# Hymba layer on one core: the last four attention heads projected as q, k, v, z, the input loaded in four pieces, and a new step table

## The chip, the cores and the metric

The kernel runs on one core of a Trainium2 chip. The metric is the time of one execution on the device in microseconds (us); lower is better.

## The reference

One layer of a model with two token mixers side by side, for one sequence of 256 tokens and 1024 channels, in float32:

```python
h = rms_norm(x, norm_w)
proj = h @ w_in                       # q_a k_a v_a z_a | qkv_dn | z_dn | b_dn a_dn
qa, ka = rms_norm(heads(q_a)), rms_norm(heads(k_a))       # 8 heads of 64
o_a = softmax(causal(qa @ ka.T / 8 + rel_bias)) @ heads(v_a)
y_a = o_a * silu(z_a)
qkv_dn = silu(causal_depthwise_conv(qkv_dn, conv_w))      # 4 heads of 128
q_d, k_d, v_d = l2_norm(q), l2_norm(k), v
beta = sigmoid(b_dn);  g = -exp(a_log) * softplus(a_dn + dt_bias)
o_d = gated_delta_rule_chunked(q_d, k_d, v_d, g, beta)
y_d = rms_norm(o_d) * silu(z_dn)
out = x + concat(y_a, y_d) @ w_out
```

The sequence is one block of the block-sparse attention, so that each query sees its own block alone, causally. The delta rule goes over chunks of tokens; this kernel uses two chunks of 128 for each of the four heads, and needs for each the inverse of a unit lower triangular matrix.

## The kernel before

**Products.** All products with weights go through one sequence on TensorE (PE), written in `products()`. It has four stretches: `z` (8 slices of the input, 12 matmuls each: z, beta and decay columns of the delta mixer), `d` (12 chunks of 24 matmuls: q, k, v of the delta mixer), `a` (8 groups of 48 matmuls: v, q, k, z of the attention heads 0 to 3, then v, q, k, z of heads 4 to 7), and `o` (the output product, 192 matmuls). Each product is made of three fp32r matmuls: weight and input are split in a rounded part (`wh`, `xh`) and a remainder (`wl`, `xl`). ScalarE (ACT) makes the rounded parts (L195, L266), VectorE (DVE) the remainders (L196, L267). Raw weights come through a pool of 4 buffers (`wr`), the two parts have 4 buffers each, so that a chunk can be split only when PE has done with the chunk four before it.

**Steps.** Everything else is written as generators: `norm`, `gates`, `bias`, `prep` and `base` (the triangular inverse, by doubling in `levels`), `scan` (the delta rule over the two chunks of a head), `heads4` (norm and transposition of q or k of four heads, named `heads` plus segment plus half: `heads01` is q of the last four heads, `heads11` their k), and `pair` (attention of two heads: scores L689, softmax L696 to L707, transposes L712, products with V L723 and L725). After each six product matmuls the sequence calls `advance()`, which counts a step and lets each generator run up to its next `yield` if its number in the table `AT` has come. So `AT` says behind which product matmul the matmuls of a step stand on PE. PE keeps the order in which the program is written. On ACT, DVE, GpSimd (POOL) and SyncE (SP, which issues the loads) a scheduler sorts the instructions, and so their order moves as well when a table entry moves. Matmul results go to the 8 banks of PSUM, which are handed out from a list as they come free.

**Lines that the steps touch.** L208 loads the input slices `px`, each before its slice of `wz`. L266 makes `xh` of a slice, L276 the squares `sq` for the norm, L288 sums them; L135 is the power on POOL that gives `rtok` and the norms `r` of q and k. L311 to L345 make the decay `g` from the product in stretch `z`; L352, L353 and L363 are the matmuls on `g`. L403 (`un`) and L407 (`cv`) are the convolution on DVE. L507 (`tm`) and L509 (`Mt`) are the 15 rounds of substitution of a `base`, L512 follows them. L552, L555 (copy of `X`) and L558 to L560 are one level of the inverse. L647, L650 and L655 (`qn`) are the norm in `heads4`. L589 to L634 are the `scan` of a head: L589 its start, L595 and L596, L610 and L611, L618, L622 its further products, L634 its transposes. L712 has the transposes of a pair, L714 the copies `pT` on ACT.

**What holds a pair.** A `pair` goes on to its products with V only when V and z of its half have been handled:

```python
while done["vz"] < 2 + 2 * (pa // 2):
    yield
```

Of the kernel before, what the change touches and what calls it, by code (L numbers as in the profile page):

```python
# [11 lines left out]
ALU = mybir.AluOpType  # L12
# [22 lines left out]
LD, LS, PRI, REP, MTL, BDK = 7, 4, 100, 16, 1, 14  # L35
OUTS = ((0, 2), (0, 0), (1, 2), (1, 0), (0, 3), (1, 3), (0, 1), (1, 1))
AT = {
    ("attention", 0): 88, ("attention", 1): 97, ("attention", 2): 128, ("attention", 3): 117, ("attention", 4): 120,
# [3 lines left out]
    ("base1", 8): 124, ("bias", 0): 0, ("bias", 1): 6, ("bias", 2): 43, ("gates", 0): 29, ("gates", 1): 35,  # L42
# [13 lines left out]
}  # L56
SEGS = (2, 0, 1, 3)
W_NORM, W_BA, W_PREP, W_BASE, W_LV, W_SC, W_Y, W_QK, W_SM, W_PT, W_HD, NP = 7, 16, 4, 34, 2, 3, 5, 6, 2, 2, 3, 2


# [1 line left out]
def tile_hymba_layer(ctx: ExitStack, tc: tile.TileContext, xt, wz, wdn, wat, wout, rb, cst, oneh, out):  # L62
# [14 lines left out]
    def rot(shape, name, tag, bufs=2, dt=F32):  # L77
        return rp.tile(shape, dt, name=name, tag=tag, bufs=bufs)
# [17 lines left out]
    def start(name, gen, wait=1):  # L96
        streams.append([gen, AT.get((name, 0), now[0] + wait), name, 0])
# [51 lines left out]
    for _ in range(NWARM):  # L149
# [11 lines left out]
    WB = 1024  # L161
    chunks = ([(f"z{i}", wz[i], ZC) for i in range(KT)]
              + [(f"d{i}", wdn[i], 1024) for i in range(12)]
              + [(f"a{s}{i}", wat[4 * s + i], 1024) for hf in range(2) for s in SEGS for i in (2 * hf, 2 * hf + 1)]
              + [(f"o{mh}{n}", wout[4 * mh + n], 1024) for mh, n in OUTS])
    raws, halves, loads, slabs = [], [], [], []

# [31 lines left out]
    def chunk(i):  # L199
        while len(raws) < min(i + LD, len(chunks)):  # L200
            load()
        while len(halves) < min(i + LS, len(chunks)):
            split()
        return halves[i]

    for k in range(KT):
        r = slice(P_COLS + k * S if k else 0, P_COLS + (k + 1) * S)
        nc.sync.dma_start(px[:, r], xt[:, r])  # L208
        load()


# [41 lines left out]
    def gemm(ps, xs, w, k, c, cols, first, last):  # L253
        xa, xb = (t[:, k, c * P:(c + 1) * P] for t in xs)
        wh, wl = w
        PE.matmul(ps, lhsT=xa, rhs=wh[:, cols], start=first, stop=False)  # L256
        PE.matmul(ps, lhsT=xb, rhs=wh[:, cols], start=False, stop=False)  # L257
        PE.matmul(ps, lhsT=xa, rhs=wl[:, cols], start=False, stop=last)  # L258

    def two(t):  # L260
        return t.rearrange("p (c d) -> p c d", c=2)
# [418 lines left out]
    def pair(pa):  # L680
# [34 lines left out]
            pTs.append(pT)  # L715
        free.append(banks[1])
        yield W_PT
        while done["vz"] < 2 + 2 * (pa // 2):
            yield

        b = banks[0]
# [21 lines left out]
    def products():  # L743
        i = 0

        def dn(ps, w, wk, k, first, last):
            PE.matmul(ps, lhsT=w[0][:, wk], rhs=xh[:, k, :], start=first, stop=False)  # L747
            PE.matmul(ps, lhsT=w[0][:, wk], rhs=xl[:, k, :], start=False, stop=False)  # L748
            PE.matmul(ps, lhsT=w[1][:, wk], rhs=xh[:, k, :], start=False, stop=last)  # L749
# [33 lines left out]
        start("attention", attention())  # L783

        n = 20
        for hf in range(2):
            cols = slice(hf * S, (hf + 1) * S)
            for seg in SEGS:
                ps = yield from grab1()
                for i in range(2):  # L790
                    w = chunk(n)
                    n += 1
                    for j in range(4):
                        k = 4 * i + j
                        for c in range(2):
                            first, last = k == 0 and c == 0, k == KT - 1 and c == 1
                            if seg == 3:

                                dn(ps[:, c * S:(c + 1) * S], w, slice(j * S + c * P, j * S + (c + 1) * P), k, first, last)
                            else:  # L800
                                gemm(ps[:, c * S:(c + 1) * S], (xh, xl), w, k, c, slice(j * S, (j + 1) * S), first, last)
                        yield
                if seg < 2:
                    start(f"heads{seg}{hf}", heads4(seg, hf, ps))
                elif seg == 2:

                    for c in range(2):
                        ACT.mul(V[:, c, cols], ps[:, c * S:(c + 1) * S], rhalf[:, c:c + 1])
                    free.append(ps)
                else:  # L810
                    if not za:
                        za.append(rot([P, 4, S], "za", "Lb", 1))
                    zs = rot([P, 2, S], f"zs{hf}", "k2", 4)
                    DVE.tensor_tensor(out=zs, in0=two(ps), in1=rbc.unsqueeze(1).to_broadcast([P, 2, S]), op=ALU.mult)
                    free.append(ps)
                    ez = rot([P, 2, S], f"ez{hf}", "k2", 4)
                    act(ez, zs, AF.Tanh, scale=0.5)
                    DVE.scalar_tensor_tensor(out=za[0][:, 2 * hf:2 * hf + 2, :], in0=ez, scalar=1.0, in1=zs, op0=ALU.add,
                                             op1=ALU.mult)
                done["vz"] += seg >= 2  # L820

        po, ot = {}, {}

# [41 lines left out]
    def grab1():  # L865
        while not free:
            yield
        return free.pop(0)
# [67 lines left out]
```

## Time and profile before

| | us |
|---|---|
| median of 3 runs | 166.14 |
| fastest, slowest | 164.9, 166.62 |
| the profiled execution, its own time | 166.0 |
| its span, from the first to the last instruction | 164.1 |
| PE busy | 156.8 |
| DVE busy | 130.3 |
| ACT busy | 103.1 |
| POOL busy | 19.8 |

The span is 1.9 us shorter than the time of the same execution. The mean granted clock of TensorE over the span is 1.000. The three runs lie 1.72 us apart, which is 1% of the time. Busy times count the time in which at least one instruction of an engine ran; matmuls overlap, so that a row of one matmul is longer than its distance from the next.

### The profile page before, as it was taken

What the parts mean: (1) busy time and instruction counts of PE and PEld (TensorE: products, weight loads), DVE (VectorE), ACT (ScalarE), POOL (GpSimd) and SP (SyncE); (2) the same over time, 40 slices, a digit from 0 to 9 for tenths busy, and PEclk for the clock granted to TensorE, in tenths of its full rate; (3) what the DMA queues carried; (4) which work ended last, traced back from release to release, by engine and by line L of the source; (5) the groups of instructions that cost most, each with busy time, mean ns of one, the idle gap of its engine ahead of it and who ended that gap; (6) DMA issues with size and microseconds to landing.
All of it is one profiled execution on the core that took longest, in us unless ns stands there. A gap on an engine that the chain in (4) does not pass through costs nothing.

```text
span 164.1 us, 4034 instructions
## 1 busy us (share of the span) xinstructions
PE 156.8 (96%) x1548; PEld 148.3 (90%) x1548; DVE 130.3 (79%) x381; ACT 103.1 (63%) x244; POOL 19.8 (12%) x29
## 2 busy tenths in 40 slices
PE   7999899999999999999999999999999979999990
PEld 7869899999999999999999989989988858999990
DVE  2569859999598999999999999987676997356261
ACT  5769497539988558787636695655657885343100
POOL 7200410000002000031230001042220010003000
PEclk9999999999999999999999999999999999999999
DMA  5999888899965327574344434434312300000033
GB/s 148 270 365 355 248 262 222 248 179 192 339 206 209 128 80 213 223 216 172 122 138 135 132 123 134 128 132 132 116 51 93 128 0 4 0 0 0 4 128 128
DMA packets 9930, 25.01 MB, mean 152 GB/s; under 512 B 1165, under 2 KB 3981, under 8 KB 9912
## 3 DMA queue, kind: packets, MB, share of 16 engines
q1 hardware_dynamic: 9208, 23.66, 46.6%
q10 hardware_dynamic: 576, 0.92, 1.5%
q8 instruction: 12, 0.20, 0.5%
q0 software_dynamic: 128, 0.18, 0.4%
q14 instruction: 6, 0.05, 0.1%
HBM read 23.52 MB, written 1.25 MB: 151 GB/s over the span
## 4 chain that ended last, share of the span: by engine, by line
PE 70%; DVE 13%; ACT 6%; DMA 3%; issue 2%; SPq 2%; POOL 1%; DVEq 0%
PE ps L256 8%; PE ps L257 7%; PE ps L258 7%; PE ps L748 6%; PE ps L749 6%; PE ps L747 6%; PE ps L836 4%; PE ps L838 4%; PE ps L837 4%; DVE wl_d L196 3%; DMA px<-xt 3%; PE ps L462 2%; DVE cv L407 2%; PE ps L689 1%; PE ps L712 1%
## 5 line engine op out<-in xcount | busy, mean ns | idle before, releaser
L256 PE MATMUL ps<-wh_a,xh 128*128 128x256 f32 x96 | 28.5, 297 | 0.0
L747 PE MATMUL ps<-xh,wh_d 128*128 128x256 f32 x96 | 27.8, 289 | 0.0
L748 PE MATMUL ps<-xl,wh_d 128*128 128x256 f32 x96 | 26.8, 280 | 0.0
L749 PE MATMUL ps<-xh,wl_d 128*128 128x256 f32 x96 | 26.8, 279 | 0.0
L257 PE MATMUL ps<-wh_a,xl 128*128 128x256 f32 x96 | 26.7, 279 | 0.0
L258 PE MATMUL ps<-wl_a,xh 128*128 128x256 f32 x96 | 26.7, 279 | 0.0
L195 ACT CAST wh_a<-wr_a 128x1024 fp32r<-128x1024 f32 x16 | 16.8, 1049 | 7.2 <-PE ps L748 3.7
L196 DVE TENSOR_TENSOR wl_a<-wr_a,wh_a 128x1024 fp32r<-128x1024 f32 x16 | 19.4, 1215 | 0.7 <-ACT wh_a L195 0.6
L256 PEld LDWEIGHTS ps<-wh_a,xh 128*128 128x128 f32 x96 | 18.1, 188 | 0.7 <-issue 0.5
L836 PE MATMUL ps<-yh,wh_o 128*128 128x256 f32 x64 | 18.7, 292 | 0.0
L257 PEld LDWEIGHTS ps<-wh_a,xl 128*128 128x128 f32 x96 | 18.1, 188 | 0.1
L258 PEld LDWEIGHTS ps<-wl_a,xh 128*128 128x128 f32 x96 | 18.1, 189 | 0.0
L748 PEld LDWEIGHTS ps<-xl,wh_d 128*128 128x128 f32 x96 | 18.1, 188 | 0.1
L747 PEld LDWEIGHTS ps<-xh,wh_d 128*128 128x128 f32 x96 | 18.0, 188 | 0.1
L407 DVE SCALAR_TENSOR_TENSOR cv<-un,px,cv 128x255 f32<-128x255 f32 (+2 forms) x36 | 16.4, 475 | 2.0 <-ACT cv L405 2.0
L749 PEld LDWEIGHTS ps<-xh,wl_d 128*128 128x128 f32 x96 | 18.0, 187 | 0.0
L837 PE MATMUL ps<-yl,wh_o 128*128 128x256 f32 x64 | 17.9, 280 | 0.0
L838 PE MATMUL ps<-yh,wl_o 128*128 128x256 f32 x64 | 17.9, 279 | 0.0
L196 DVE TENSOR_TENSOR wl_d<-wr_d,wh_d 128x1024 fp32r<-128x1024 f32 x12 | 14.6, 1214 | 1.2 <-ACT wh_d L195 1.1
L195 ACT CAST wh_d<-wr_d 128x1024 fp32r<-128x1024 f32 x12 | 12.6, 1052 | 2.4 <-PE ps L748 1.9
L196 DVE TENSOR_TENSOR wl_o<-wr_o,wh_o 128x1024 fp32r<-128x1024 f32 x8 | 9.8, 1221 | 3.6 <-ACT wh_o L195 3.6
L836 PEld LDWEIGHTS ps<-yh,wh_o 128*128 128x128 f32 x64 | 12.0, 188 | 0.5 <-issue 0.3
(210 smaller groups left out, 406.7 us busy)
## 6 DMA issues: line engine op xcount, KB each, us to landing
wr_a<-wat SPq DMA_DIRECT2D x16, 512.0 KB, 3.3
wr_d<-wdn SPq DMA_DIRECT2D x12, 512.0 KB, 5.6
wr_o<-wout SPq DMA_DIRECT2D x8, 512.0 KB, 3.3
wr_z<-wz SPq DMA_DIRECT2D x7, 260.0 KB, 5.8
T<-bd SPq DMA_DIRECT2D x8, 128.0 KB, 5.8
px<-xt SPq DMA_DIRECT2D x7, 128.0 KB, 4.9
out_t<-ot ACTq DMA_DIRECT2D x3, 256.0 KB, 2.4
cs<-cst SPq DMA_DIRECT2D x1, 192.0 KB, 4.9
```

Source lines behind the costliest of these rows:

```text
L195: ACT.copy(h[:, r], raw[:, r])
L196: eng.tensor_tensor(out=l[:, r], in0=raw[:, r], in1=h[:, r].bitcast(F32), op=ALU.subtract)
L256: PE.matmul(ps, lhsT=xa, rhs=wh[:, cols], start=first, stop=False)
L257: PE.matmul(ps, lhsT=xb, rhs=wh[:, cols], start=False, stop=False)
L258: PE.matmul(ps, lhsT=xa, rhs=wl[:, cols], start=False, stop=last)
L407: DVE.scalar_tensor_tensor(out=a[:, 3 - j:], in0=src[:, 0:S - 3 + j], scalar=pr[:, o + j:o + j + 1], in1=a[:, 3 - j:], op0=ALU.mult, op1=A ...
L747: PE.matmul(ps, lhsT=w[0][:, wk], rhs=xh[:, k, :], start=first, stop=False)
L748: PE.matmul(ps, lhsT=w[0][:, wk], rhs=xl[:, k, :], start=False, stop=False)
L749: PE.matmul(ps, lhsT=w[1][:, wk], rhs=xh[:, k, :], start=False, stop=last)
L836: PE.matmul(ps, lhsT=w[0][:, o], rhs=yh[:, k, :], start=(first and j == 0 and (m % 2 == 0 or alone)), stop=False)
L837: PE.matmul(ps, lhsT=w[0][:, o], rhs=yl[:, k, :], start=False, stop=False)
L838: PE.matmul(ps, lhsT=w[1][:, o], rhs=yh[:, k, :], start=False, stop=(last and j == 1 and (m % 2 == 1 or alone)))
```

## The change

Three things. The input is loaded in four pieces of two slices each (one `px` load ahead of every second `wz` load) instead of eight. The eight groups of stretch `a` are listed one by one in `SEGS`: v, q, k, z of the first four heads as before, then q, k, v, z of the last four, instead of v, q, k, z. The counter `done["vz"]` is replaced by a note for each group. And most numbers of the table `AT` are new.

```diff
-    ("base0", 0): 40, ("base0", 1): 100, ... ("gates", 0): 29, ("gates", 1): 35, ... ("heads01", 1): 120,
-    ... ("heads11", 1): 127, ... ("pair2", 0): 111, ... ("pair3", 0): 144, ... ("bias", 1): 6, ...
+    ("base0", 0): 40, ("base0", 1): 102, ... ("gates", 0): 27, ("gates", 1): 33, ... ("heads01", 1): 113,
+    ... ("heads11", 1): 118, ... ("pair2", 0): 121, ... ("pair3", 0): 138, ... ("bias", 1): 3, ...
-SEGS = (2, 0, 1, 3)
+SEGS = ((2, 0), (0, 0), (1, 0), (3, 0), (0, 1), (1, 1), (2, 1), (3, 1))
...
     for k in range(KT):
-        r = slice(P_COLS + k * S if k else 0, P_COLS + (k + 1) * S)
-        nc.sync.dma_start(px[:, r], xt[:, r])
+        if k % 2 == 0:
+            r = slice(P_COLS + k * S if k else 0, P_COLS + (k + 2) * S)
+            nc.sync.dma_start(px[:, r], xt[:, r])
         load()
...
-        while done["vz"] < 2 + 2 * (pa // 2):
+        while (2, pa // 2) not in done or (3, pa // 2) not in done:
             yield
...
-        for hf in range(2):
+        for seg, hf in SEGS:
             cols = slice(hf * S, (hf + 1) * S)
-            for seg in SEGS:
-                ps = yield from grab1()
+            ps = yield from grab1()
...
-                done["vz"] += seg >= 2
+            done[seg, hf] = 1
```

What this does to the order of instructions is shown at three places. From the loads on, lines of the changed file are two higher than before (L345 is now L347, L555 is L557, L712 is L714), and one higher behind the loop over `SEGS` (L836 is L837).

**At the start**, ACT had `xh` of slice 0, then both parts of `wh_z0`, and then the squares of slices 0 and 1. Now the first two slices arrive as one piece, and ACT has `xh`, the squares (128x512), `xh` of slice 1, and only then `wh_z0`. The later loads of `px` alternate with two loads of `wz` each.

**DVE ahead of the decay `g`** (stretch `d`; `wl_d` are remainders of weight chunks, `cv` and `un` belong to the convolution, `rs` and `ln` lead to `g`). Before:

```order
L196 TENSOR_TENSOR wl_d_436<-wr_d_338,wh_d_435 128x1024
L343 TENSOR_TENSOR ln_484<-ln_484,rs_486 128x8
L407 SCALAR_TENSOR_TENSOR cv_389<-un_390,px,cv_389 128x253
L407 SCALAR_TENSOR_TENSOR cv_426<-un_427,px,cv_426 128x255
L345 TENSOR_TENSOR g<-ln_484,eal 128x2x4
L403 TENSOR_TENSOR un_499<-ps_78,rbc 128x256
L196 TENSOR_TENSOR wl_d_508<-wr_d_356,wh_d_507 128x1024
```

Now:

```order
L196 TENSOR_TENSOR wl_d_432<-wr_d_334,wh_d_431 128x1024
L342 TENSOR_TENSOR rs_470<-rs_470,ua 128x8
L409 SCALAR_TENSOR_TENSOR cv_422<-un_423,px,cv_422 128x255
L409 SCALAR_TENSOR_TENSOR cv_385<-un_386,px,cv_385 128x253
L344 TENSOR_TENSOR rs_470<-xa,rs_470 128x8
L409 SCALAR_TENSOR_TENSOR cv_422<-un_423,px,cv_422 128x254
L196 TENSOR_TENSOR wl_d_504<-wr_d_352,wh_d_503 128x1024
L405 TENSOR_TENSOR un_495<-ps_78,rbc 128x256
L345 TENSOR_TENSOR ln_468<-ln_468,rs_470 128x8
L409 SCALAR_TENSOR_TENSOR cv_422<-un_423,px,cv_422 128x253
L347 TENSOR_TENSOR g<-ln_468,eal 128x2x4
L405 TENSOR_TENSOR un_548<-ps_74,rbc 128x256
```

The first row is the same weight chunk in both; the next chunk's `wl_d` stood behind `g` and now stands ahead of it. On PE the matmuls on `g` (L352, L353 and the first four of L363) stand two steps, twelve product matmuls, earlier than before; the second four of L363 stand where they stood.

**DVE around the copy of `X`** (L555 of `base0`, which L558 on PE waits for; the `tm` and `Mt` rows are rounds of `base1`). Before:

```order
L507 TENSOR_TENSOR tm_1279<-Lb_1277,Mt_152 128x4x6
L509 TENSOR_TENSOR Mt_152<-Mt_152,tm_1279 128x2x2x6
L196 TENSOR_TENSOR wl_a_1571<-wr_a_1366,wh_a_1570 128x1024
L507 TENSOR_TENSOR tm_1279<-Lb_1277,Mt_152 128x4x5
L509 TENSOR_TENSOR Mt_152<-Mt_152,tm_1279 128x2x2x5
L555 COPY X_1600<-ps_73 32x128
L507 TENSOR_TENSOR tm_1279<-Lb_1277,Mt_152 128x4x4
```

Now:

```order
L509 TENSOR_TENSOR tm_1275<-Lb_1273,Mt_148 128x4x7
L196 TENSOR_TENSOR wl_a_1565<-wr_a_1362,wh_a_1564 128x1024
L511 TENSOR_TENSOR Mt_148<-Mt_148,tm_1275 128x2x2x7
L657 TENSOR_TENSOR qn_1614<-ps_71,r_1612 128x512
L509 TENSOR_TENSOR tm_1275<-Lb_1273,Mt_148 128x4x6
L557 COPY X_1594<-ps_72 32x128
L511 TENSOR_TENSOR Mt_148<-Mt_148,tm_1275 128x2x2x6
```

The `qn` of q of the last four heads (L657), and further up its reduction (L649, 128x512) and its small L652, now stand ahead of the copy of `X`, where before they came after all of `base1`; of the rounds of `base1` three `tm` or `Mt` fewer stand ahead of it. On PE the transposes of that `qn` move from behind the 720th product matmul of the kernel to behind the 672nd, where L558 stands too; those of k move from 756 to 702.

**PE in the middle of stretch `o`**, behind the 792nd product matmul, where pair 3 has its attention and the scans of heads 0 and 3 go on (`pb4` to `pb7` and `pT4` to `pT7` are heads 4 to 7, `ps6_77` and the like are PSUM banks). Before, the scores of pair 3 stand behind L610, L611 (scan 0) and L589, and behind the scores come:

```order
L712 MATMUL ps5_76<-cs_97,pb4_1970 128x128 x3
L712 MATMUL ps2_73<-cs_97,pb5_1971 128x128 x3
L618 MATMUL ps1_72<-r10_2026,MT_150 128x128
L723 MATMUL ps5_76<-pT4_2057,V_157 64x256
L723 MATMUL ps5_76<-pT5_2062,V_157 64x256
L725 MATMUL ps5_76<-pT4_2057,V_157 64x128
L725 MATMUL ps5_76<-pT5_2062,V_157 64x128
L622 MATMUL ps1_72<-v10_2065,aT_143 128x128
L595 MATMUL ps7_78<-v0d3_2032,ktok_144 128x128
L596 MATMUL ps7_78<-v03_2031,aT_143 128x128
L712 MATMUL ps6_77<-cs_97,pb6_2039 128x128 x3
L712 MATMUL ps4_75<-cs_97,pb7_2040 128x128 x3
```

Now the scores of pair 3 come first, and behind them:

```order
L620 MATMUL ps4_75<-r10_2000,MT_146 128x128
L714 MATMUL ps7_78<-cs_97,pb4_1842 128x128 x3
L714 MATMUL ps5_76<-cs_97,pb5_1843 128x128 x3
L591 MATMUL ps1_72<-vt_141,MT_146 128x128
L624 MATMUL ps4_75<-v10_2046,aT_139 128x128
L725 MATMUL ps7_78<-pT4_2051,V_153 64x256
L725 MATMUL ps7_78<-pT5_2056,V_153 64x256
L727 MATMUL ps7_78<-pT4_2051,V_153 64x128
L727 MATMUL ps7_78<-pT5_2056,V_153 64x128
L714 MATMUL ps3_74<-cs_97,pb6_2030 128x128 x3
L714 MATMUL ps6_77<-cs_97,pb7_2031 128x128 x3
L597 MATMUL ps1_72<-v0d3_2060,ktok_140 128x128
```

The two products L595 and L596 of scan 3, which stood ahead of the transposes of pair 3, now stand behind them, L589 of scan 3 now stands behind the scores, and L610 and L611 of scan 0 have left the place for one 18 product matmuls earlier. On DVE the four scalings L707 of pair 3 now follow each other directly; before, a `yl` stood between the third and the fourth.

Elsewhere: the scores of pair 2 move from behind product matmul 768 to 720, the bias matmul (L381) from 36 to 18, the steps of `prep0` 12 product matmuls later, and on ACT the first `ba` (L311) and the four `zd` now stand behind the third `wh_d` instead of the second.

## Rows read from the trace of the kernel before

**Rows 1.** The page: the span, and section 1, busy time by engine.

```profile
span 164.1 us, 4034 instructions
PE 156.8 (96%) x1548; PEld 148.3 (90%) x1548; DVE 130.3 (79%) x381; ACT 103.1 (63%) x244; POOL 19.8 (12%) x29
```

**Rows 2.** Waits of PE, the largest: waiter <- releaser: us in total, times, longest.

```profile
PE ps L712 <- DVE pb L707: 1.2, 2, 0.9
```

**Rows 3.** Busy time by stretch: us, PE, PEld, DVE, ACT, POOL, clock, DMA share, GB/s.

```profile
4.00:11.00 7.00, 6.82 (x40) 5.86 (x39) 3.95 (x10) 4.65 (x10) 1.07 (x3) 1.00 0.95 308
```

**Rows 4.** PE timeline of stretch z: start, us, line and operation, [idle before <-releaser].

```profile
4.05 0.56 PE L256 MATMUL ps<-wh_z,xh 128*128 128x256 f32 x1
...
6.83 0.44 PE L256 MATMUL ps<-wh_z,xh 128*128 128x256 f32 x1
...
11.95 0.39 PE L258 MATMUL ps<-wl_z,xh 128*128 128x256 f32 x1 [0.23 <-DVE wl_z L196]
...
20.30 0.28 PE L747 MATMUL ps<-xh,wh_d 128*128 128x256 f32 x1
```

**Rows 5.** ACT timeline of the start.

```profile
3.00 0.51 ACT L266 ACTIVATE xh<-px 128x256 fp32r<-128x256 f32 x1 [1.00 <-DMA px<-xt]
...
5.14 0.63 ACT L276 ACTIVATE sq<-px 128x512 f32<-128x512 f32 x1 [0.16 <-DMA px<-xt]
5.68 0.49 ACT L266 ACTIVATE xh<-px 128x256 fp32r<-128x256 f32 x1
```

**Rows 6.** DMA issues, 4 to 11 us: count, KB each, median us to landing.

```profile
wr_z<-wz SPq DMA_DIRECT2D x5, 260.0 KB, 5.9
px<-xt SPq DMA_DIRECT2D x5, 128.0 KB, 5.7
```

**Rows 7.** DMA issue of the fourth input slice, in the window 3.97 to 4.3 us.

```profile
px<-xt SPq DMA_DIRECT2D x1, 128.0 KB, 5.5
```

**Rows 8.** DVE timeline around the decay `g`.

```profile
28.54 1.22 DVE L196 TENSOR_TENSOR wl_d<-wr_d,wh_d 128x1024 fp32r<-128x1024 f32 x1
...
29.76 0.87 DVE L407 SCALAR_TENSOR_TENSOR cv<-un,px,cv 128x253 f32<-128x253 f32 x2
30.55 0.16 DVE L345 TENSOR_TENSOR g<-ln,eal 128x8 f32<-128x8 f32 x1
30.62 0.41 DVE L403 TENSOR_TENSOR un<-ps,rbc 128x256 f32<-128x256 f32 x1
```

**Rows 9.** PE timeline: the first matmul on `g`.

```profile
33.47 0.28 PE L352 MATMUL ps<-g,cs 128*128 128x8 f32 x2
```

**Rows 10.** DVE timeline around the copy of `X` and the norm of q.

```profile
102.18 0.18 DVE L507 TENSOR_TENSOR tm<-Lb,Mt 128x20 f32<-128x20 f32 x1
...
102.61 0.30 DVE L555 COPY X<-ps 32x128 f32<-32x128 f32 x1
...
106.75 0.64 DVE L647 TENSOR_REDUCE s<-sqa 128x8 f32<-128x512 f32 x1
...
111.47 0.69 DVE L655 TENSOR_TENSOR qn<-ps,r 128x512 f32<-128x512 f32 x1 [1.07 <-POOL r L135]
```

**Rows 11.** PE timeline: the level of the inverse behind the copy of `X`.

```profile
103.28 0.21 PE L558 MATMUL ps<-X,MT 32*32 32x32 f32 x1
```

**Rows 12.** POOL timeline: the power for q of the last four heads.

```profile
108.95 2.48 POOL L135 TENSOR_TENSOR r<-s,mhalf 128x8 f32<-128x8 f32 x1 [9.25 <-DVE s L650]
```

**Rows 13.** Busy time behind product matmul 792, columns as above.

```profile
128.93:137.79 8.86, 7.69 (x60) 5.62 (x59) 8.10 (x34) 7.13 (x22) 0.69 (x1) 1.00 0.15 53
```

**Rows 14.** PE timeline of the same stretch.

```profile
129.69 0.93 PE L689 MATMUL ps<-kT,qT 64*128 64x128 f32 x8
...
133.16 0.39 PE L595 MATMUL ps<-v0d,ktok 128*128 128x128 f32 x2
...
134.68 0.81 PE L712 MATMUL ps<-cs,pb 128*128 128x128 f32 x4 [0.91 <-DVE pb L707]
...
136.01 0.39 PE L610 MATMUL ps<-S,kq 128*128 128x128 f32 x2
```

More of the change, by code (lines that the diff above doesn't have):

```diff
@@ L37 @@
 AT = {
-    ("attention", 0): 88, ("attention", 1): 97, ("attention", 2): 128, ("attention", 3): 117, ("attention", 4): 120,
[3 rows of a table removed]
-    ("base1", 8): 124, ("bias", 0): 0, ("bias", 1): 6, ("bias", 2): 43, ("gates", 0): 29, ("gates", 1): 35,
[13 rows of a table removed]
+    ("attention", 0): 88, ("attention", 1): 100, ("attention", 2): 117, ("attention", 3): 111,
[4 rows of a table added]
+    ("gates", 0): 27, ("gates", 1): 33, ("gates", 2): 36, ("gates", 3): 49, ("heads00", 0): 75, ("heads00", 1): 96,
[12 rows of a table added]
 }
-SEGS = (2, 0, 1, 3)
+SEGS = ((2, 0), (0, 0), (1, 0), (3, 0), (0, 1), (1, 1), (2, 1), (3, 1))
 W_NORM, W_BA, W_PREP, W_BASE, W_LV, W_SC, W_Y, W_QK, W_SM, W_PT, W_HD, NP = 7, 16, 4, 34, 2, 3, 5, 6, 2, 2, 3, 2
@@ L163, in tile_hymba_layer @@
               + [(f"d{i}", wdn[i], 1024) for i in range(12)]
-              + [(f"a{s}{i}", wat[4 * s + i], 1024) for hf in range(2) for s in SEGS for i in (2 * hf, 2 * hf + 1)]
+              + [(f"a{s}{i}", wat[4 * s + i], 1024) for s, hf in SEGS for i in (2 * hf, 2 * hf + 1)]
               + [(f"o{mh}{n}", wout[4 * mh + n], 1024) for mh, n in OUTS])
@@ L785, in products @@
         n = 20
-        for hf in range(2):
+        for seg, hf in SEGS:
             cols = slice(hf * S, (hf + 1) * S)
-            for seg in SEGS:
-                ps = yield from grab1()
[L790 to L805, printed above, removed]
-                    for c in range(2):
[L808 to L819, printed above, removed]
-                done["vz"] += seg >= 2
@@ new lines, in products @@
+            ps = yield from grab1()
+            for i in range(2):
+                w = chunk(n)
+                n += 1
+                for j in range(4):
+                    k = 4 * i + j
+                    for c in range(2):
+                        first, last = k == 0 and c == 0, k == KT - 1 and c == 1
+                        if seg == 3:
+                            dn(ps[:, c * S:(c + 1) * S], w, slice(j * S + c * P, j * S + (c + 1) * P), k, first, last)
+                        else:
+                            gemm(ps[:, c * S:(c + 1) * S], (xh, xl), w, k, c, slice(j * S, (j + 1) * S), first, last)
+                    yield
@@ new lines, in products @@
+            if seg < 2:
+                start(f"heads{seg}{hf}", heads4(seg, hf, ps))
+            elif seg == 2:
+                for c in range(2):
+                    ACT.mul(V[:, c, cols], ps[:, c * S:(c + 1) * S], rhalf[:, c:c + 1])
+                free.append(ps)
+            else:
+                if not za:
+                    za.append(rot([P, 4, S], "za", "Lb", 1))
+                zs = rot([P, 2, S], f"zs{hf}", "k2", 4)
+                DVE.tensor_tensor(out=zs, in0=two(ps), in1=rbc.unsqueeze(1).to_broadcast([P, 2, S]), op=ALU.mult)
+                free.append(ps)
+                ez = rot([P, 2, S], f"ez{hf}", "k2", 4)
+                act(ez, zs, AF.Tanh, scale=0.5)
+                DVE.scalar_tensor_tensor(out=za[0][:, 2 * hf:2 * hf + 2, :], in0=ez, scalar=1.0, in1=zs, op0=ALU.add,
+                                         op1=ALU.mult)
```

32 rows, old and new, of the table AT are left out of this document.

## The prediction

> **What bounds the kernel now.** I read the busy times first, then the waits, then the places that the change moves. PE is busy 156.8 of 164.1 us, DVE 130.3 [rows 1]: the product sequence is the bound, and an edit counts only where it lengthens or shortens PE's work or its waits. The change takes no matmul out. The largest wait by name is that of the pair transposes L712 for the scalings L707, 1.2 us in two waits, the longest 0.9 [rows 2]. What can be won is therefore small: that wait, the time lost at the start, and small stalls. What can be lost is open, since every moved step can stop the in-order PE.
>
> The pace of the products is read from two rows: between the first matmul of stretch d at 20.30 [rows 4] and L352 at 33.47 [rows 9] stand 108 product matmuls, so 13.17 / 108 = 0.122 us each at the full clock. At the start the distance is (6.83 - 4.05) / 12 = 0.23 us [rows 4]: TensorE runs at the lower of its two levels (1.2 GHz) there, after the warm-up matmuls, and at the higher (2.4 GHz) from 6.9 on.
>
> **Part A, the start.** Now ACT makes the first `xh` at 3.00, and the first product matmul comes at 4.05, 1.05 later [rows 4, 5]. The first piece is 128 KB larger; at the 308 GB/s of the next stretch [rows 3] that is 0.42 us. Ahead of `wh_z0` ACT now also does the squares (0.54 from one start to the next, 5.14 to 5.68 [rows 5]) and a second `xh` (shown 0.49, some 0.42 to the next start). So the first product matmul moves to 4.05 + 0.42 + 0.54 + 0.42 = 5.4, and PE pauses for some 0.7 us or more after its warm-up.
>
> Against that stands where the third slice starts. Its weights arrive behind the same bytes as today's fourth input slice (1326 KB either way), which was issued at 3.98 and took 5.5 us [rows 7]: 9.5. The cast takes 0.6, so that the third slice starts at 10.25 whatever the first two do, if these are done. At the lower clock they take 24 x 0.23 = 5.5 us from 5.4, to 10.9; at the higher, less. From 10.25 there are 72 matmuls at 0.12 (8.6) with 0.9 of waits as now (one of 0.23 stands at 11.95 [rows 4]): 19.8; from 10.9 with a few matmuls more at the lower clock, 20.5. Now it is 20.30. So A is -0.5 to +0.4, and I take -0.2: the pause is short beside the time that the warm-up has run, so I lean to a clock that rises nearly as it does now. The eight loads that became four save SP four issues; I cost them at nothing, because the DMA engines are 95% busy in 4 to 11 us [rows 3] and set the time of arrival.
>
> The Trainium skill says in "DMA: Bandwidth & Descriptors", section Bandwidth, that one should batch DMAs to at least 1 MiB for 75% of the peak, which would make the larger loads faster in themselves. The rows speak against it here: with the queues full, 128 KB took 5.7 us and 260 KB 5.9 [rows 6], so the queue ahead and not the size of a load sets its arrival; by the rule the sum would come out lower, as the third rival has it.
>
> **Part B, the gates.** L352 waits for `g`. From `wl_d` at 28.54 to `g` at 30.55 DVE now needs 2.01 us [rows 8]. The order puts more ahead of `g`: one more `wl_d`, whose issue to issue time is 1.14 (1.22 less the overlap of 0.08), one `un` of 0.33, two more `cv` of 0.40 each (two take 30.55 - 29.76 = 0.79), and two `rs` of 0.08: 2.42 together. So `g` starts at 32.97 and is there at 33.07, if DVE reaches the same `wl_d` at the same time, which I take since that chunk's turn is set by PE's pace as now. PE reaches L352 twelve matmuls earlier, at 33.47 - 1.46 = 32.0, and waits 1.06. Today `g` is there almost 3 us before it is used. The twelve product matmuls come behind the wait on the same in-order engine and cannot hide it. What is queued behind: all products, and with them every later release of weight buffers. If part A brings PE 0.2 earlier, the wait grows by as much, so that A and B together are +1.0. Bounds: `g` cannot come much before 32.0, since the extra `wl_d` needs a buffer that PE frees 36 matmuls before today's L352 (29.1), and the cast (1.05), `wl_d`, `un` and one `cv` come behind that: no wait at the lower end. At the upper end DVE is half a `cv` chain later: +1.5. With A's own bounds A and B are -0.5 to +1.5. The later `ba` on ACT costs nothing as long as `g` hangs on the extra `wl_d`.
>
> **Part C, the last four heads' q and k.** L558 at 103.28 [rows 11] comes 0.37 after the end of the copy of `X` (102.61 + 0.30 [rows 10]), so the cover is some 0.3. Ahead of the copy stand now the reduction (0.64 shown, 0.57 to the next), `qn` (0.69, 0.62) and a small one (0.08), and three rounds' halves fewer at 0.215 each, from 102.18 and 102.61: 1.27 - 0.64 = +0.63 [rows 10]. The copy ends 0.63 later, and PE waits about 0.35. DVE's chain behind it is longer too, and `base1` ends about when PE wants it: 0.05. The transposes of q and k fall in with work that they now precede and cost what they did. C = +0.4. Lower bound 0, if DVE gets there earlier because less stands ahead elsewhere; upper +1.2, from the rival below.
>
> **Part D, attention of pair 3.** Now the place takes 8.86 us, of which PE is busy 7.69 [rows 13]; the scores come at 129.69 and the transposes at 134.68 [rows 14], 4.99 us later, with ACT (a weight cast, exponentials, copies `pT`, a scan's scalings) and DVE between. The changed order has the same kinds of instructions between, so I keep 4.99. What changes: the scores come at once instead of 129.69 - 128.93 = 0.76 in; the six transposes take about 0.9 instead of 136.01 - 134.68 = 1.33, since the four L707 follow each other and the second, 0.3 us wait [rows 2] goes; behind them stand the same scan products, `pT` and V products as now (137.79 - 136.01 = 1.78) plus L595 and L596 (0.44 by two pairs at 0.22). Sum 4.99 + 0.9 + 1.78 + 0.44 = 8.11; L610 and L611 (0.44) run elsewhere: 8.55 against 8.86, -0.3. With less PE work between scores and transposes the wait itself becomes longer, not shorter; the gain comes from starting the chain earlier. I take -0.3. Bounds: -1.3 if ACT gets through 0.9 sooner, which would remove the wait that is now 0.9; +0.5 if a `pT` copy or a cast comes between.
>
> **The rest.** The steps of `prep0` 12 matmuls later, the scores of pair 2 48 earlier, the bias 18 earlier: each is a move of the same matmuls to a place where their inputs are long there or their results not yet wanted. I cost them at nothing; the output stretch at the end is unchanged.
>
> **The sum.** A and B +1.0, C +0.4, D -0.3: +1.1 against the profiled execution's 166.0, so 167.1. The median is 166.14, and the three runs lie 1% apart; about 1% (1.7 us) is what a measurement can tell from no change, so the forecast, 0.6% above the median, lies within it.
>
> **Rivals.**
> 1. Faster. No new wait arises: DVE is ahead in d because less stands ahead of it than I think, the input lands earlier, and the chain of pair 3 loses its wait. A -0.5, B 0, C 0, D -1.3: -1.8, 164.2. For it: each of the places was a wait before [rows 2, 4]. Against it: B's count of instructions ahead of `g` is plain. Chance 0.22.
> 2. Slower. The copy of `X` now stands behind `qn`, which waits for POOL's power `r`. Now `qn` waited 1.07 us for it, and the power took 2.48 [rows 10, 12]. It decides from the point at which `r` ends later than DVE reaches `qn`, at about 102.3: with the power starting at 101 instead of 99.5, `qn` is 1.1 to 1.3 late, and L558, and with it all products, wait as long on top of C: 168.2. For it: two long operations on two engines now stand in one chain with PE at its end. Against it: between the reduction and `qn` the order has on DVE one `wl_a` (1.14) and nine halves of rounds (1.9), some 3 us, in which the power can run. Chance 0.28.
> 3. Larger loads are faster in themselves. If the bytes ahead of the third slice's weights came a quarter faster than 308 GB/s [rows 3], they would land 1.1 us earlier (a fifth of the 5.5 [rows 7]), DVE's work in z and d would move up by some 0.7 with it, and A and B fall to +0.3: with C and D 166.4, within 1% too. Chance 0.1; the Trainium skill's rule above is its ground, [rows 6] speak against it.
> The forecast itself has 0.4.
>
> **How the numbers follow.** Range: the bounds of the parts sum to -1.8 and +3.2, but they will not all fall on one side. The lower end takes in rival 1, 164.2; the upper end goes 0.4 over rival 2, 168.6. Faster by over 1% means below 164.5: most of rival 1, 0.19. Slower by over 1% means above 167.8: rival 2 and a little of the forecast's own upper half, 0.29. Within 1%: 0.52.
>
> **What would show it.** A: the first product matmul at about 5.4, the start of d between 19.8 and 20.5. B: L352 with a wait of 1 us on `g`, which ends at about 33. C: a wait of L558 for the copy of `X` of some 0.4, with `qn` just ahead of that copy and without a wait on POOL. D: scores to transposes still about 5 us, one wait instead of two, and the place 8.1 us long. The prediction is wrong if `g` comes before PE wants it, if the clock stays at its lower level for longer than the first two slices, or if a bank or buffer is freed late in a place that I have costed at nothing.

## The result, and the profile after

The changed kernel takes 166.44 us (median of 20 runs, 165.04 to 167.28), the kernel before 165.34 us (20 runs, 164.6 to 166.62): a ratio of 1.0057, 95% interval 1.0038 to 1.0077. It is slower by 0.6%, some 0.9 to 1.1 us; the forecast was +1.1 us, 0.7% on the profiled execution's 166.0. The total is right. Its parts are not: the start and the gates cost less than half of what the sum had for them, the norm of q and k about twice as much, and of the gain of 0.3 in the attention of pair 3 only some 0.1 came.

The page of the changed kernel, its first lines, against [rows 1]:

```profile
span 164.6 us, 4028 instructions
PE 156.1 (95%) x1548; PEld 147.6 (90%) x1548; DVE 130.6 (79%) x381; ACT 103.4 (63%) x244; POOL 18.9 (11%) x29
```

The busy times are as before; what is new is in the waits of PE (against [rows 2]; columns: us in total, times, longest):

```profile
PE ps L258 <- ACT wh_z L195: 1.0, 1, 1.0
PE ps L714 <- DVE pb L709: 0.9, 1, 0.9
PE ps L560 <- DVE X L557: 0.6, 1, 0.6
PE ps L354 <- DVE g L347: 0.4, 1, 0.4
PE ps L725 <- ACT pT L716: 0.4, 1, 0.4
```

Each of the four parts has its wait: 1.0 ahead of the first product (A), 0.4 on `g` (B), 0.6 on the copy of `X` (C), and in pair 3 the second wait of L712 is gone, but one of 0.4 for `pT` has come (D).

To see what each wait does to the end, I counted product matmuls in the timeline of PE and read the time at which the n-th starts. "Again" is a second profiled execution of the changed kernel. The order of products alone (below) has the same instructions as before up to about the 624th, so that its first columns are a second execution of the kernel before.

| product matmul | 0 | 96 (d) | 216 | 624 | 768 | last ends |
|---|---|---|---|---|---|---|
| before | 4.05 | 20.30 | 37.51 | 94.71 | 125.78 | 160.09 |
| order of products alone | 4.05 | 19.84 | 36.66 | 93.80 | 125.47 | 159.78 |
| changed kernel | 5.37 | 20.05 | 37.53 | 94.89 | 126.79 | 161.05 |
| changed kernel, again | 5.37 | 20.11 | 37.58 | 94.28 | 126.19 | 160.38 |

Two executions of the same instructions differ by 0.9 us at the 624th matmul (94.71 and 93.80), and 0.6 in the changed kernel. So A and B can only be read as means over several profiles, while the stretches behind repeat to about 0.1: from 624 to 768 the kernel before takes 31.07, the changed one 31.90 and 31.91; from 768 to the end 34.31 against 34.26 and 34.19. PE has as many other matmuls in either stretch before as after (368 and 80), so that these differences are waits and order, not work.

### The profile page after: what moved, and what is told of

It reads as the page before. It is cut to its first block, busy times and chain, and to the rows that moved or that the text cites. A ratio compares the mean times of both kernels' runs of the same rounds, so it can differ in the third digit from the quotient of the medians.

```text
span 164.6 us, 4028 instructions
## 1 busy us (share of the span) xinstructions
PE 156.1 (95%) x1548; PEld 147.6 (90%) x1548; DVE 130.6 (79%) x381; ACT 103.4 (63%) x244; POOL 18.9 (11%) x29
## 4 chain that ended last, share of the span: by engine, by line
PE 66%; DVE 16%; DMA 7%; ACT 4%; issue 3%; SPq 2%; ACTq 0%; DVEq 0%
PE ps L749 7%; PE ps L750 7%; PE ps L751 7%; PE ps L258 5%; PE ps L839 5%; PE ps L260 5%; PE ps L259 5%; PE ps L838 5%; PE ps L837 5%; DMA px<-xt 4%; DMA wr_d<-wdn 3%; DVE wl_a L196 3%; DVE wl_d L196 3%; PE ps L464 2%; PE ps L725 2%
## 5 line engine op out<-in xcount | busy, mean ns | idle before, releaser
L837 PE MATMUL ps<-yh,wh_o 128*128 128x256 f32 x64 | 18.6, 290 | 0.0
L195 ACT CAST wh_o<-wr_o 128x1024 fp32r<-128x1024 f32 x8 | 8.4, 1046 | 6.3 <-PE ps L838 4.4
```

Of the source, the lines that this page charges most:

```text
L195: ACT.copy(h[:, r], raw[:, r])
L837: PE.matmul(ps, lhsT=w[0][:, o], rhs=yh[:, k, :], start=(first and j == 0 and (m % 2 == 0 or alone)), stop=False)
```

## The experiments

**1. The order of the products alone**: loads and step table of before, the list `SEGS` and the notes of the changed kernel.

> The new order of the products (q, k, v, z of the last four heads) and the notes for each group, with the loads and the step table of before. On DVE the norm of q stands ahead of the copy of X, as in the changed kernel; g stands ahead of the extra weight remainder, as before. Theory C (the norm of q ahead of the copy of X is what makes the changed kernel slower): PE waits some 0.4 to 0.7 us for that copy, and the time is 0.5 to 1.0 us above before. Rival B (the wait for g, 0.4 us in the changed kernel): no wait for g here, and the time is within 0.3 us of before.

Measured: 165.54 us, ratio to before 1.001 (0.9981 to 1.0039). The wait for the copy of `X` is there, with the table of before:

```profile
PE ps L713 <- DVE pb L708: 1.2, 2, 0.9
PE ps L150 <- DVE ones L139: 1.0, 1, 1.0
PE ps L559 <- DVE X L556: 0.5, 1, 0.5
```

From 624 to 768 it takes 31.67, 0.60 more than before. So it is the order q, k, v, z that puts the norm of q ahead of `X`, not the table. That its time is not 0.5 us higher fits neither theory well; the interval reaches to +0.65 us, and its profiled execution reached the 624th matmul 0.9 us before that of before.

**2. The step table alone**: loads and order of products of before.

> The new step table alone, with the loads and the order of the products of before. On DVE g stands behind the extra weight remainder, and the copy of X has no norm of q ahead of it. Theory C: no wait for the copy of X, so the time is within 0.4 us of before, with a wait for g of 0.4 to 0.7 us that the second group of matmuls on g gives back. Rival B: the wait for g stays in the end time, 0.5 us or more above before.

Measured: 179.59 us, ratio 1.08. The table has the transposes of q at a step at which the old order has not yet made q: L663 waits 8.7 us for `qn`, in two waits. Up to there the run can be read: L352 waits 0.4 us for `g`, and d starts at 20.27, the 216th matmul at 37.74, the 624th at 94.37, 0.34 before the row of before. The gates' wait does not show at the end of that stretch. The table and the order belong together; the time of this run says nothing on either theory.

**3. The loads alone**:

```diff
     for k in range(KT):
-        r = slice(P_COLS + k * S if k else 0, P_COLS + (k + 1) * S)
-        nc.sync.dma_start(px[:, r], xt[:, r])
+        if k % 2 == 0:
+            r = slice(P_COLS + k * S if k else 0, P_COLS + (k + 2) * S)
+            nc.sync.dma_start(px[:, r], xt[:, r])
         load()
```

> The four loads of two slices alone, with all else as before. If the input's part is as it looks in the changed kernel, the first product matmul comes 1.3 us later and stretch d starts 0.2 to 0.3 us earlier, and the time is 0.2 to 0.3 us below before. Rival (the earlier start of d comes from the bias step that moved, not from the loads): d starts no earlier than before, and the time is the same or up to 0.5 us higher.

Measured: 171.17 us, ratio 1.0315 (1.0266 to 1.0364). On the time both were wrong by far (that d starts no earlier the rival had right), and most of the loss lies 90 us behind the loads:

```profile
PE ps L559 <- DVE X L556: 1.9, 1, 1.9
...
PE ps L553 <- ACT MT L545: 1.0, 1, 1.0
PE ps L530 <- DVE Mp L513: 0.8, 1, 0.8
```

The scheduler, which sorts DVE's instructions by its own estimate of times, has given another order around the copy of `X` when only the loads changed: the end of `base1` and a weight remainder now stand ahead of it. At the start, d begins at 20.90, later than before; what goes with that is shown with the next run.

**4. The norm of q behind the copy of `X`**: an order without a wait between the two DVE instructions, and the transposes of q three steps later (116 instead of 113).

```diff
-        DVE.tensor_copy(X32[q3], b32[q3, 0])
+        xcopy.append(DVE.tensor_copy(X32[q3], b32[q3, 0]))
...
-        DVE.tensor_tensor(out=qn.rearrange(...), ...)
+        i = DVE.tensor_tensor(out=qn.rearrange(...), ...)
+        if (seg, hf) == (0, 1):
+            after(i, xcopy[0])
```

> The changed kernel with the norm qn of q of the last four heads put behind the copy of X on DVE, and its transposes on PE three steps later. Theory C: the copy of X comes 0.6 us earlier, the wait of PE for it falls from 0.6 to 0.1 or less, and the time falls by 0.4 to 0.6 us against the changed kernel, to 0.4 to 0.6 us above before. Rival (DVE is so full there that the work only changes places): the wait moves to the transposes of qn or to base1 behind, and the time stays within 0.2 us of the changed kernel.

Measured: 170.3 us, ratio 1.0247. The wait for `X` is gone: from 624 to 672 the run takes 8.98, against 9.89 in the changed kernel, of which the wait was 0.6 (the rest goes with the four transposes of q, which now stand behind the 672nd). But the scheduler then put the first remainder of the output weights and the norm of k between the last transpositions of `base1`, PE waited 0.3 us for `Mp` and 1.0 for `MT`, and lost more than these. The stretches of this run (us, PE, PEld, DVE, ACT, POOL busy, granted clock, DMA share, GB/s):

```profile
108.00:110.00 2.00, 1.65 (x55) 1.34 (x54) 1.93 (x6) 1.84 (x4) 1.28 (x1) 1.00 0.59 231
110.00:112.00 2.00, 0.92 (x10) 0.59 (x9) 1.89 (x5) 0.00 (x0) 0.00 (x0) 1.00 0.21 53
112.00:114.00 2.00, 1.89 (x68) 1.39 (x70) 0.81 (x4) 0.21 (x1) 0.57 (x2) 0.74 0.61 217
114.00:116.00 2.00, 2.00 (x14) 1.30 (x11) 0.71 (x2) 0.62 (x2) 0.00 (x0) 0.50 0.00 0
```

PE was idle for about 1.4 us between 108 and 112, and from some point in 112 to 114 the granted clock fell to 0.50, the lower level (1.2 GHz), until after 116: from the 696th to the 720th matmul this run needs 11.46 us, the changed kernel 8.07. Of these 3.4 us the wait for `MT` is 1.0 (that for `Mp` stands ahead of the 696th); the rest lies where the clock was low. That the idle time made the clock fall is not shown: in run 9 PE was idle for longer, and it did not fall.

The start of this run, which has the instructions of the changed kernel, shows the lower level at another place. Its first products, and then those of the changed kernel:

```profile
5.44 0.58 PE L258 MATMUL ps<-wh_z,xh 128*128 128x256 f32 x1 [1.05 <-ACT wh_z L195]
5.82 0.41 PE L259 MATMUL ps<-wh_z,xl 128*128 128x256 f32 x1
...
8.31 0.41 PE L258 MATMUL ps<-wh_z,xh 128*128 128x256 f32 x1
```

```profile
5.37 0.38 PE L258 MATMUL ps<-wh_z,xh 128*128 128x256 f32 x1 [1.00 <-ACT wh_z L195]
5.59 0.28 PE L259 MATMUL ps<-wh_z,xl 128*128 128x256 f32 x1
...
6.13 0.28 PE L258 MATMUL ps<-wh_z,xh 128*128 128x256 f32 x1
```

A matmul that shows 0.41 runs at the lower level, one of 0.28 at the higher. Behind the same pause of 1 us the first slice runs at either: of the eight profiled executions with four loads and this pause three (runs 3, 4 and 12) ran it, and at least half of the second slice, at the lower level and began d at 20.85 to 20.90, the five others (the changed kernel, runs 5, 7, 9 and 11) at 19.55 to 20.13.

**5. The changed kernel again**, unaltered.

> The changed kernel once more, unaltered. Theory (the clock at the start differs between executions: in the profiled execution of the changed kernel the first slice ran at the full clock, in the run with the norm of q put behind the copy of X, whose start is the same, at half): this profile has either the start of stretch d at 20.0 to 20.2 or at 20.8 to 21.0, and the wait of 0.6 us for the copy of X in both cases. Rival (the start is fixed by the order of the instructions): stretch d starts at 20.05 again. The time is 0.6% above before either way.

Measured: 166.66 us, ratio 1.0069 (1.0048 to 1.0091); d at 20.11, wait for `X` 0.6. The two levels at the start are shown by the runs together, not by this one.

**6. A longer warm-up**: `NWARM` 9 instead of 7.

> The changed kernel with nine warm-up matmuls instead of seven, so that they end at about 5.2 us, where the first product matmul can start, instead of 4.4; the order of all other instructions is that of the changed kernel. Theory (the pause of 1 us ahead of the first product matmul lets the clock stay low in some executions): the first slice runs at the full clock, stretch d starts at 19.9 to 20.1, and the time is 0.2 to 0.6 us below the changed kernel. Rival (the bytes of the third slice set the start of d): no change of the time, within 0.2 us.

Measured: 166.05 us, ratio 1.0043 (1.0021 to 1.0066), 0.26% below run 5. The pause is gone (the first product still starts at 5.38), the first slice is at the higher level, d begins at 20.03. The sign is that of the theory, but the intervals of runs 5 and 6 overlap: inconclusive.

**7. The norm of q behind `X`, the rest held in place**: as run 4, and the first `wl_o` and the norm of k ordered behind the last transposition of `base1`, in the same manner.

> The changed kernel with the norm of q behind the copy of X on DVE, and the first remainder of the output weights and the norm of k held behind the last transposition of base1, so that the order behind is as in the changed kernel. Theory C: no wait for the copy of X, no wait at the next level of base1, no drop of the clock behind it, and the time is 0.4 to 0.8 us below the changed kernel. Rival (DVE is full in this stretch, and the wait only moves): a wait of 0.4 us or more in slots behind, the time within 0.2 us of the changed kernel.

Measured: 166.13 us, ratio 1.0046 (1.0021 to 1.0071). No wait for `X`, no drop of the clock, but

```profile
PE ps L534 <- DVE Mp L516: 0.4, 1, 0.4
```

at the first product of `base1`. From 624 to 768: 31.81, 0.09 below the changed kernel. The rival was right for the stretch: the wait moved. The time is 0.23% below run 5, which is nearer to the theory's 0.4 to 0.8 us than to the rival's 0.2, but the intervals overlap. In this execution d began early, at 19.55, and the wait for `g` is the longest of all:

```profile
PE ps L356 <- DVE g L349: 1.0, 1, 1.0
```

`g` came at 32.13, as in the changed kernel, and the 216th matmul at 37.57 against 37.53: what PE was ahead, it waited off at `g`.

**8. The order of products alone, with the norm of q behind `X`** (run 1 with the edits of run 7).

> The new order of the products with the loads and table of before, and the norm of q put behind the copy of X as in the run before. Theory C: the wait of 0.5 us that the new order of products alone had is gone, and the time is 0.2 to 0.6 us below before. Rival: the wait moves to base1 behind and the time stays as before, within 0.2 us.

Measured: 166.53 us, ratio 1.0067 (1.0041 to 1.0092). The wait for `X` went, and one of 0.7 us for `Mp` came; 624 to 768 took 32.35, 1.28 more than before, and the time is 1.1 us above before. Worse than run 1, and neither theory nor rival had it. Theory C in its first form, that the place of one instruction is the cause, fell with runs 7 and 8. The form that I tested next: DVE has too much work up to the end of `base1`, and the order only decides which product waits.

**9 and 10. One remainder on POOL**: `PW = (34,)`, the second last chunk of stretch a, in the changed kernel and in run 1.

> The changed kernel with one weight remainder, that of the second last chunk of stretch a, made on POOL instead of DVE: 1.14 us less DVE work ahead of the norm of q, the copy of X and the end of base1; PE needs that chunk some 13 us later. Theory (DVE has too much work between the scores and the end of base1, and where the wait shows is a matter of order): the wait for the copy of X goes and none comes in its place, PE is 0.5 to 0.7 us earlier from there on, and the time is 0.4 to 0.8 us below the changed kernel. Rival (the cost lies in the order q ahead of X alone, or POOL gets in the way of DVE): the time stays within 0.2 us of the changed kernel.

> The new order of the products with loads and table of before, and the same remainder on POOL. Theory: its wait of 0.5 us for the copy of X goes without another in its place, and the time is 0.3 to 0.6 us below that of the new order of products alone, which was 0.1% above before; this would be the version that beats both. Rival: POOL's work slows DVE or its own power for the norms, and the time is as before or above.

Measured: 168.31 us (ratio 1.0178) and 168.84 us (ratio 1.0172). The wait for `X` rose to 2.3 and 2.0 us. DVE of run 9, then its POOL:

```profile
101.20 0.18 DVE L511 TENSOR_TENSOR Mt<-Mt,tm 128x24 f32<-128x24 f32 x1
101.42 2.24 DVE L509 TENSOR_TENSOR tm<-Lb,Mt 128x20 f32<-128x20 f32 x1
103.69 0.69 DVE L657 TENSOR_TENSOR qn<-ps,r 128x512 f32<-128x512 f32 x1
```

```profile
99.64 1.64 POOL L135 TENSOR_TENSOR r<-s,mhalf 128x8 f32<-128x8 f32 x1
101.25 2.37 POOL L196 TENSOR_TENSOR wl_a<-wr_a,wh_a 128x1024 fp32r<-128x1024 f32 x1
```

A `tm` that takes 0.2 us elsewhere took 2.24, to the end of POOL's subtraction at 103.62. PE stood still meanwhile for 2.3 us within 4, and its granted clock (the figure behind POOL's busy time) stayed at 1.00:

```profile
102.00:104.00 2.00, 0.54 (x5) 0.33 (x3) 1.97 (x2) 1.90 (x4) 1.62 (x1) 1.00 0.00 0
104.00:106.00 2.00, 1.15 (x31) 1.11 (x32) 1.77 (x9) 0.08 (x2) 0.00 (x0) 1.00 0.69 223
```

In run 10 a `tm` took 2.28 in the same way; behind the wait of 2.0 the clock was 0.81 from 104 to 106 and 0.50 from there to 108, so that part of that run's loss is the clock. The rivals' mechanism held, POOL gets in DVE's way, though the time of run 9 is far beyond the 0.2 us that its rival gave. The Trainium skill, "GPSIMD Engine Reference", section Specifications, lists POOL's access to SBUF as shared with VectorE, with contention when a DVE instruction has two inputs in SBUF; this `tm` has two, and the run agrees. It is not so beside every POOL instruction: the `Mt` and `tm` that ran beside the power at 99.64 took 0.17 to 0.20 each.

**11. The gates where they were**: the four `gates` entries of before in the changed table.

> The changed kernel with the steps of the gates of before: L354 and the first matmuls on g stand twelve product matmuls later again, while DVE still has the extra weight remainder ahead of g. Theory (g comes at 32.1 to 32.4 and PE passes L354's old place at 33.2): no wait for g, and the product matmul behind the gates comes 0.4 us earlier than in the changed kernel; what follows on DVE is sorted anew, so the end time may differ. Rival (the wait for g only stands where another wait, for the second group of matmuls on g or for a free bank, would stand): no gain of time at the 240th product matmul.

Measured: 171.42 us, ratio 1.0347 (1.031 to 1.0384). No wait for `g`; the 240th matmul starts at 40.19, against 40.36 and 40.41 in the changed kernel, and the 336th at 54.17 against 54.71 and 54.59: 0.2 to 0.5 us. Behind that the new order loses more: L440 waits 1.6 us for `kq` and L665 2.1 for `qn`, and from 90 to 94 the granted clock is at 0.59 and 0.56. So the gates' wait costs some 0.2 to 0.5 us where it stands (one execution), and its step alone, moved back in this table, costs more elsewhere.

**12. Less DVE work**: run 7, with the remainder of the second last chunk of stretch a left out (its products take the remainder of the chunk before).

> As the second run with the norm of q behind the copy of X, and one remainder of stretch a (the second last chunk) is not computed at all: its products use the remainder of the chunk before, so one of DVE's 1.14 us operations is left out and its output lacks that correction. Theory (the amount of DVE work up to the end of base1 is what PE waits for, in whatever order): no wait for the copy of X and none for the first product of base1, and from the 624th to the 768th product matmul PE loses at most 0.3 us against before, where that run lost 0.74; the time is 0.4 to 0.6 us below that run. Rival (the wait is due to places on PE, not to DVE's amount): PE loses 0.6 us or more there again.

Measured: no wait for `X` and none for `Mp`, 31.24 from 624 to 768 (before 31.07, run 7 31.81): 0.57 less than run 7 for 1.14 us less on DVE. The three smallest of its waits on PE, where L534 <- `Mp` stood in run 7:

```profile
PE ps L358 <- DVE g L351: 0.4, 1, 0.4
PE ps L734 <- ACT pT L725: 0.4, 1, 0.4
PE ps L559 <- ACT MT L551: 0.3, 1, 0.3
```

Its time is 165.62 us, ratio 1.0026 (1.0003 to 1.0049), 0.20% below run 7 where 0.4 to 0.6 us were expected; the intervals overlap. The stretch shows what the theory says, the total only leans that way. In this run the norm of q also stood later among the rounds, so that the effect is that of one operation less together with the order that followed from it.

No run beat both kernels; run 1 equals the kernel before within its interval.

## Why the prediction was right, point by point

**A, the start** (-0.2 taken, -0.5 to +0.4). The first product came at 5.37 (5.4 foretold), d at 20.05 and 20.11 (about 20.1). The times came out; two of the reasons did not. I took the pause to leave the clock's rise nearly where it was, behind the first slice. It does so in none of the eight executions of run 4's count: in five the second product already runs at the higher level, and d is reached at 20.1 or earlier; in three the lower level lasts into the second slice, and d comes at 20.9, 0.4 beyond my upper bound. And I let the weights of the third slice arrive at 9.5. In the changed kernel ACT casts them at 8.28, without a wait for the load:

```profile
8.28 0.61 ACT L195 CAST wh_z<-wr_z 128x520 fp32r<-128x520 f32 x1
```

The third slice began at 10.00, close to my 10.25, because PE had the first two to finish until then, not because of its weights. As a mean over the eight profiles d begins at 20.28, over four with the old loads and table (20.30, 19.84, 20.05 and 20.02, of before and runs 1, 8 and 10) at 20.05: +0.2 where I had -0.2, less than the spread of either group.

**B, the gates** (+1.06 for the wait; A and B together +1.0). Wrong in size: the wait was 0.43 (0.4 to 0.6 in six executions with these instructions, 1.0 in run 7). `g` came at 32.09, not at 32.97, and the step that failed is "if DVE reaches the same `wl_d` at the same time". The counts behind that `wl_d` were right; the `wl_d` itself began at 27.67 instead of 28.54. The DVE rows of the changed kernel:

```profile
20.84 1.23 DVE L196 TENSOR_TENSOR wl_d<-wr_d,wh_d 128x1024 fp32r<-128x1024 f32 x1 [1.33 <-ACT wh_d L195]
...
27.67 1.22 DVE L196 TENSOR_TENSOR wl_d<-wr_d,wh_d 128x1024 fp32r<-128x1024 f32 x1
...
32.09 0.15 DVE L347 TENSOR_TENSOR g<-ln,eal 128x8 f32<-128x8 f32 x1
```

and the PE row that waits:

```profile
32.39 0.36 PE L354 MATMUL ps<-g,cs 128*128 128x8 f32 x2 [0.43 <-DVE g L347]
```

The first of these is the third `wl_d`. Before, it stood at 22.71, because DVE waited there for a cast that ACT made only after `ba` and `zd`:

```profile
22.71 1.22 DVE L196 TENSOR_TENSOR wl_d<-wr_d,wh_d 128x1024 fp32r<-128x1024 f32 x1 [1.07 <-ACT wh_d L195]
```

I had listed that move of `ba` behind the third `wh_d` and asked only what a later `ba` costs. The other half of the swap, a cast that comes earlier and with it a DVE chain that runs ahead, is what I left out. The explanation is read from traces; no run moved `ba` alone. Nor is the lead always 0.9. In the four executions with the instructions of before (before, runs 1, 8 and 10) the third `wl_d` stands at 21.48 to 22.71 and the sixth, the one I counted from, 5.8 behind it; in seven with those of the changed kernel (its own, runs 4, 5, 6, 7, 9 and 12) the third stands at 20.41 to 21.02, always earlier, but the sixth at 27.37 to 28.15. The profile that I read has the latest sixth of its four, run 1 the earliest:

```profile
27.32 1.22 DVE L196 TENSOR_TENSOR wl_d<-wr_d,wh_d 128x1024 fp32r<-128x1024 f32 x1
```

Between the means of the two groups the sixth is 0.3 earlier, not 0.9: part of the missed size lies in the one execution that I counted from. Run 7 shows the coupling of A and B that the sum had: there d began 0.5 earlier, and the wait was 0.5 longer. At the 624th matmul the six executions with the changed kernel's instructions up to there (its own, runs 4, 5, 7, 9 and 12) have a mean of 94.55, the four of before and runs 1, 8 and 10 94.26: A and B together +0.3, with a spread of 0.9 to 1.1 in either group. That is less than the +1.0 of the sum, and hardly to be told from nothing.

**C, q and k** (+0.4 taken, 0 to +1.2). The mechanism was right, the size half: the stretch from 624 to 768 is 0.83 longer, and 0.61 of that is the wait for `X`. DVE and PE of the changed kernel:

```profile
97.65 1.21 DVE L196 TENSOR_TENSOR wl_a<-wr_a,wh_a 128x1024 fp32r<-128x1024 f32 x1
...
98.87 0.68 DVE L649 TENSOR_REDUCE s<-sqa 128x8 f32<-128x512 f32 x1
...
102.82 0.69 DVE L657 TENSOR_TENSOR qn<-ps,r 128x512 f32<-128x512 f32 x1
...
103.64 0.30 DVE L557 COPY X<-ps 32x128 f32<-32x128 f32 x1
```

```profile
103.99 0.21 PE L560 MATMUL ps<-X,MT 32*32 32x32 f32 x1 [0.61 <-DVE X L557]
```

The copy ends 1.03 later than in [rows 10], not 0.63. I had credited three half rounds that no longer stand ahead of it; but from the weight remainder at 97.6 on, which is where DVE stands at the same time in both kernels (97.57 and 97.65), only one fewer stands before it. The other two had been displaced further up, where they gave nothing back. The second term that I set at 0.05, the end of `base1`, was not a small rest but the other end of the same chain: runs 7 and 8 show that the wait goes to whichever of the two products comes first behind DVE's added 1.3 us.

**D, pair 3** (-0.3 taken, -1.3 to +0.5). PE of the changed kernel, against [rows 13, 14]:

```profile
130.38 0.38 PE L691 MATMUL ps<-kT,qT 64*128 64x128 f32 x2
...
133.33 0.43 PE L725 MATMUL ps<-pT,V 128*64 128x256 f32 x1 [0.37 <-ACT pT L716]
...
135.51 1.16 PE L714 MATMUL ps<-cs,pb 128*128 128x128 f32 x6 [0.92 <-DVE pb L709]
136.51 0.39 PE L597 MATMUL ps<-v0d,ktok 128*128 128x128 f32 x2
```

Scores to transposes take 5.13 (4.99 foretold), the six transposes 1.00 with no second wait (0.9), and the place ends at 138.78, 8.4 us after the scores began, where I had 8.1. The products with V now wait 0.37 for `pT` on ACT, which I had named only as an upper bound. From 768 to the end the gain is 0.05 to 0.12. It comes with the table: this stretch takes 34.30 to 34.31 in the five executions with the table of before, whatever the loads and the order of products, and 34.19 to 34.26 in the nine with the new one.

**The rivals.** The faster one fell with B and C. The slower one fell on its condition: the power for q ran from 100.47 to 102.11 in the changed kernel, 0.7 ahead of `qn` at 102.82, which had no wait on POOL. For the third, the bytes did not come faster (305 GB/s from 4 to 11 us, before 308), and d begins no sooner with the four loads; that the third slice's weights still came ahead of my 9.5 moved nothing, since PE was not waiting for them.

**The sum** was A and B +1.0, C +0.4, D -0.3; the traces give +0.3, +0.8 and -0.1. Two errors of about 0.7 and 0.4 in opposite directions made a total that is right, and that is luck. What the forecast had right is where PE would wait and for what, the wait for `pT` apart; the sizes, and the clock at the start, it had wrong.

## What to carry to other kernels

When an order swaps two operations, price both halves: who waits longer for the one that moved back, and who runs ahead because of the one that moved up. A time read from one execution carries that execution's luck: the sixth `wl_d` differed by 1.2 us between four executions of the same instructions, more than the wait that was counted from it. When work is added to an engine that is busy without a pause, count from the last point at which it stands at the same time in both orders; where the wait then shows is a matter of order, and pushing one instruction aside moves it, while less work took it away (run 12). In a kernel whose other engines are sorted by a scheduler, a table, an order of products and the loads are one setting: the table alone, the loads alone, one norm moved and the gates' steps moved back (runs 2, 3, 4 and 11) were each 2.5 to 8% above before, mostly at places that the edit did not touch; the order of products alone (run 1) cost nothing that its interval shows.

## What the runs showed of the hardware that I had not expected

- A `tensor_tensor` of 128x1024 on POOL (2.37 us) held a DVE operation of 128x20 for 2.24 us instead of 0.2 (run 9; 2.28 in run 10), while the power on 128x8 on POOL (1.64 us) left DVE's like operations beside it at 0.2.
- In the middle of the kernel the granted clock went to 0.50 for over 2 us behind 1.4 us of idle time within 4 us (run 4), and stayed at 1.00 behind 2.3 us of idle time within 4 us (run 9): the length of the idle time alone did not decide.
- Behind the same pause of 1 us at the start, the first slice ran at the lower level in three of eight profiled executions and at the higher in five; d began at 20.85 to 20.90 in the three, at 20.13 or earlier in the five.
